# Where the operands of the matmuls lie in SBUF: moving tiles at 416 modulo 1024, weight parts at 0 modulo 1024

## The chip, the core and the metric

The kernel runs on one core of one Trainium2 chip. The metric is the device time of one execution in microseconds. Before the change three runs took 1342.55, 1343.47 and 1345.52 us; the median is 1343.47.

## What is computed

Two layers of a decoder trunk on 256 tokens of width 1024, batch 1, all in float32. Each layer:

```python
h = h + 0.5 * swiglu(rms_norm(h), ffn1)                  # 1024 -> 2 x 2816 -> 1024
u = rms_norm(h)
parts = split(u @ w_in)                                  # q, k, v, gates of four mixers
ys = (gated_deltanet, mlstm, s5_ssm, moba_attention)     # each 256 wide
h = h + sum_b(sigmoid(u @ w_gate[b]) * (ys[b] @ w_branch[b])) @ w_out
h = h + 0.5 * swiglu(rms_norm(h), ffn2)
h = h + (p[i] @ w_ple) * sigmoid(rms_norm(h) @ w_ple_gate)
```

and a final RMSNorm. Most of the arithmetic is in the dense products with w_gu, w_down, w_in, w_gate, w_branch, w_out and w_ple. With 256 tokens each weight is used once per execution, so all weights (some 230 MB) are read from HBM once.

## The kernel before

**Layout.** Activations stand transposed: channels on the 128 partitions, the 256 tokens along the free axis. A dense product takes a 128x128 block of weights as TensorE's stationary operand and a 128x256 block of activations as its moving operand, and writes a 128x256 block of PSUM. For the few products whose result is wanted with tokens on the partitions (`proj_t`: z, av, mv, mo) the roles are swapped: a block of activations is stationary and a block of weights moves.

**Three matmuls for one product.** A float32 number is split in a high part that the fast fp32r format holds exactly and a low part, the rest. A product is then high x high + high x low + low x high, three fp32r matmuls, in `mm3`:

```python
mm(out, w[0], x[0], start=start, stop=False)   # wh stationary, x high moves
mm(out, w[0], x[1], start=False, stop=False)   # wh again, x low moves
mm(out, w[1], x[0], start=False, stop=stop)    # wl stationary, x high moves
```

Every matmul loads its own stationary block (LDWEIGHTS), so there are as many loads as matmuls.

**Weights.** `unit` brings 512 KB of weights with one DMA into a tile `raw` (128 x 1024 float32, 4 buffers); ScalarE casts it into `wh`, VectorE subtracts and writes `wl` (6 buffers each). A block of 128 columns is 512 bytes of a partition's row, so in a unit the eight blocks begin at the tile's start and every 512 bytes after it.

**Moving tiles.** `xa` (two constants, high and low, 8 blocks each) holds the normalised input of a feed-forward network or of the mixers; `A` holds the gated hidden block of a feed-forward network (input of w_down); `B` the merged mixer output (input of w_out), the input of the ple gate and one mixer's result; `Y` and `D` the results of the other mixers, `Y` also the ple embedding. Each 128x256 block is 1024 bytes long, and blocks of a tile follow one another, so all blocks of one tile name begin at the same address modulo 1024.

**The feed-forward loop** (`ffn`): for each of 22 blocks f of the hidden width, 48 matmuls with `xa` moving (gate and up: 2 outputs x 8 blocks x 3), then, two blocks late, 24 matmuls with `A` moving (down: 8 outputs x 3). It runs twice per layer.

**Order.** The kernel records every operation, and a planner (`Plan.order`) puts them in order with a cost per instruction, due times and the number of buffers per tag; `Plan.issue` then emits them all from one line, L427 of the profile. The planner does not know addresses. Its only trace of them is in `cost`, where an fp32r matmul gets 7 ns on top of its columns if the moving tile is `xa`, else 11.

**Addresses.** Tiles are laid out pool by pool in the order in which the pools are opened, in a pool by first use. Before, the order is: 16384 bytes of scratch for DMA descriptors, the constants (`xa` among them), the weights, then all work tiles.

Of the kernel before, what the change touches and what calls it, by code (L numbers as in the profile page):

```python
# [9 lines left out]
F = mybir.dt.float32  # L10
R = mybir.dt.float32r
# [5 lines left out]
T = 256  # L17
D = 1024
KD = D // 128
# [26 lines left out]
def constants():  # L46
# [35 lines left out]
    for name in CONSTS:  # L82
# [3 lines left out]
        parts.append(a)  # L86
    return np.concatenate(parts, axis=1), off


COLS = {"n1": (0, 8), "nm": (8, 8), "n2": (16, 8), "np": (24, 8), "conv": (32, 40), "gb": (72, 1), "alog": (73, 1),  # L90
        "bglu": (74, 2), "d5": (76, 8)}
# [8 lines left out]
BUFS = dict(A=4, B=8, C=8, D=8, T=4, Y=4, M=4, th=4, q=8, sg=2, sq=2, nacc=2, rs=2, tiny=6, rcol=2, s5prm=1, s5s=16,  # L100
            s5pw=1, s5u=2, mv=1, cols=1, gnw=1, mnw=1, sm8=16)


class Store:


    def __init__(self, pool, shape, dt, tag, bufs, bank):
        self.pool, self.shape, self.dt, self.tag, self.bufs, self.bank = pool, shape, dt, tag, bufs, bank
        self.real, self.place, self.end, self.left, self.log = None, None, 0.0, 0, []
# [121 lines left out]
class Plan:  # L231
# [89 lines left out]
    def order(self):  # L321
# [13 lines left out]
        while True:  # L335
            best = None
            for e in names:
                if ready[e]:
                    t = free[e]
                elif later[e]:  # L340
                    t = max(free[e], later[e][0][0])
                else:
                    continue
                if best is None or t < best[0]:
                    best = (t, e)
            if best is None:
                break
            t, e = best
            while t >= tick + TICK:
                warm, count, tick = count >= COLUMNS, 0.0, tick + TICK  # L350
# [54 lines left out]
            for s in v.stores:  # L405
                s.left -= 1
                s.end = max(s.end, v.end + OUT[e])
                if s.left == 0:
                    key = (id(s.pool), s.tag)
                    heapq.heappush(places[key], s.end)  # L410
                    for u in stuck.pop(key, []):
                        u.ready = max(u.ready, t)
                        known(u)
# [60 lines left out]
class Trunk:  # L474
    def __init__(self, ctx, tc, ins, out, off, where):
        self.where = where
        self.tc, self.nc, self.ins, self.out = tc, Plan(tc), ins, out
        E = ctx.enter_context
        self.cp = E(tc.tile_pool(name="const", bufs=1))
        self.wp = E(tc.tile_pool(name="weights", bufs=1))  # L480
        self.tp = E(tc.tile_pool(name="work", bufs=1))
        self.pp = E(tc.tile_pool(name="psum", bufs=1, space=bass.MemoryType.PSUM))
        self.dp = E(tc.tile_pool(name="scratch", bufs=1, space=bass.MemoryType.DRAM))
        nc = self.nc
        self.zr = self.const([128, 128], R, "zr")
        nc.gpsimd.memset(self.zr.bitcast(F), 0.0)
        n = DEPTH * NCOL
        self.xc = self.const([128, n + KD * T], F, "xc")
        self.cols = self.xc[:, 0:n].rearrange("p (l c) -> p l c", l=DEPTH)
        self.h = self.xc[:, n:].rearrange("p (k t) -> p k t", k=KD)  # L490
        self.xa = [self.const([128, KD, T], R, f"xa{j}") for j in range(2)]
        self.start()
        cst = self.const([128, sum(w for _, w in off.values())], F, "cst")
        nc.sync.dma_start(cst[:, 0:128], ins["consts"][:, 0:128])
        self.fcol = self.const([128, KD], F, "fcol")
        with nc.later():
            nc.sync.dma_start(cst[:, 128:], ins["consts"][:, 128:])
            nc.sync.dma_start(self.fcol, ins["final"])
        self.c = {k: cst[:, a:a + w] for k, (a, w) in off.items()}
        self.ident = self.c["ident"]  # L500
        V, P = nc.vector, nc.gpsimd
        self.halfs = self.const([128, 16], F, "halfs")
        P.memset(self.halfs[:, 0:8], -0.5)
        P.memset(self.halfs[:, 8:16], 0.5)
        self.meancol = self.const([128, 1], F, "meancol")
        P.memset(self.meancol, 1.0 / D)
        self.bias = self.const([128, 2], F, "bias")
        P.memset(self.bias[:, 0:1], HALF_PI)
        P.memset(self.bias[:, 1:2], EPS)
        self.pick = self.const([128, 8], R, "pick")  # L510
        with nc.later():
            nc.scalar.copy(self.pick, self.c["pick"])
# [37 lines left out]
        return self.nc.tile(self.pp, shape, F, tag, BANKS[tag], True)  # L550

    def t(self, tag, shape, dt=F):
        return self.nc.tile(self.tp, shape, dt, tag, BUFS[tag])

    def col(self, i, name):
        a, w = COLS[name]
# [1122 lines left out]
```

## Time and profile before

| | |
|---|---|
| median of three runs | 1343.47 us |
| the profiled execution | 1343.09 us |
| its span, first to last instruction | 1341.3 us |
| TensorE busy | 1321.4 us, 99% |
| weight loads busy (beside the matmuls) | 1300.2 us, 97% |
| VectorE, ScalarE, GpSimd busy | 1003.4, 738.7, 39.2 us |
| DMA | 233.67 MB, 174 GB/s in the mean |
| mean granted TensorE clock | 0.994 |

How to read it: the rows further down are of this one execution. PE is TensorE's matmuls, PEld its weight loads, DVE VectorE, ACT ScalarE. A tile pair such as `mm<-A,wh` is the output and its inputs, for a matmul the moving and the stationary tile. Matmuls overlap in the pipeline and their ends are modelled, so the mean length of one is far more than the time from one start to the next; how fast a stream of matmuls runs is seen from a window that holds nothing else, its length divided by the number of matmuls that start in it.

### The profile page before, as it was taken

How to read it: one execution, taken by the hardware profiler on the slowest of the kernel's cores; microseconds unless marked ns; L12 is line 12 of the kernel's file. 1: busy time of each engine (PE TensorE's matmuls, PEld its weight loads, DVE VectorE, ACT ScalarE, POOL GpSimd, SP SyncE). 2: the span in 40 equal slices, each digit the busy share in tenths (PEclk: the TensorE clock that was granted, in tenths of full speed). 3: DMA queues.
4: the chain of work that ended last, by engine and by line, in shares of the span. 5: the costliest groups of instructions: out<-in, count | busy, mean ns of one | idle time of the engine just before them, and what ended most of it. 6: DMA issues, size and time to landing. Idle time of an engine off the chain costs nothing.

```text
span 1341.3 us, 27989 instructions
## 1 busy us (share of the span) xinstructions
PE 1321.4 (99%) x11366; PEld 1300.2 (97%) x11366; DVE 1003.4 (75%) x1893; ACT 738.7 (55%) x1174; POOL 39.2 (3%) x73
## 2 busy tenths in 40 slices
PE   8999999999999999999999999999989999999997
PEld 8999999988999999999999999999989999999997
DVE  7998567987858765556899966778886777555575
ACT  7645457974455544444664454689635455444453
POOL 2000000000010000000020000000000100000000
PEclk9999999998999999999999999999999999999999
DMA  8665555435735655555576645553456356566551
GB/s 296 193 193 163 190 189 173 142 119 115 214 109 178 192 184 189 190 191 200 167 214 190 193 153 189 175 179 103 136 155 205 117 180 194 194 194 192 192 166 60
DMA packets 81761, 233.67 MB, mean 174 GB/s; under 512 B 20832, under 2 KB 24928, under 8 KB 81632
## 3 DMA queue, kind: packets, MB, share of 16 engines
q1 hardware_dynamic: 81632, 231.88, 55.0%
q8 instruction: 89, 1.46, 0.5%
q14 instruction: 40, 0.33, 0.1%
HBM read 229.49 MB, written 2.36 MB: 173 GB/s over the span
## 4 chain that ended last, share of the span: by engine, by line
PE 90%; DMA 3%; issue 2%; ACT 2%; DVE 1%; SPq 0%; POOL 0%; DVEq 0%; POOLq 0%; ACTq 0%
PE mm L427 64%; PE acc L427 19%; PE inv L427 7%; DMA raw<-in_weights 2%; DVE wl L427 1%; ACT wh L427 1%; DMA q<-dx 1%; DMA raw<-dm 0%; SPq L427 0%; DMA xc<-in_x 0%; ACT B L427 0%; ACT C L427 0%; DMA dx<-sg 0%; DVE th L427 0%; DVE D L427 0%
## 5 line engine op out<-in xcount | busy, mean ns | idle before, releaser
L427 PE MATMUL mm<-xa,wh 128*128 128x256 f32 x4288 | 755.4, 279 | 0.4 <-ACT wh L427 0.3
L427 ACT CAST wh<-raw 128x1024 fp32r<-128x1024 f32 (+1 forms) x434 | 437.1, 1038 | 471.4 <-issue 223.0
L427 PEld LDWEIGHTS mm<-xa,wh 128*128 128x128 f32 x4288 | 652.8, 189 | 3.9 <-ACT wh L427 1.0
L427 PE MATMUL mm<-xa,wl 128*128 128x256 f32 x2144 | 597.0, 278 | 0.8 <-DVE wl L427 0.8
L427 DVE TENSOR_TENSOR wl<-raw,wh 128x1024 fp32r<-128x1024 f32 (+1 forms) x434 | 514.2, 1207 | 54.1 <-ACT wh L427 52.9
L427 PEld LDWEIGHTS mm<-xa,wl 128*128 128x128 f32 x2144 | 405.0, 189 | 2.4 <-DVE wl L427 1.4
L427 DVE TENSOR_TENSOR T<-mm,rs 128x512 f32<-128x512 f32 x98 | 67.4, 689 | 168.6 <-PE mm L427 167.1
L427 PE MATMUL acc<-A,wh 128*128 128x256 f32 x1056 | 190.8, 280 | 1.7 <-ACT A L427 1.7
L427 PEld LDWEIGHTS acc<-A,wh 128*128 128x128 f32 x1056 | 161.2, 188 | 2.1 <-ACT A L427 1.9
L427 PE MATMUL acc<-A,wl 128*128 128x256 f32 x528 | 147.2, 280 | 0.0
L427 PE MATMUL mm<-B,wh 128*128 128x256 f32 x576 | 105.1, 283 | 0.0
L427 PEld LDWEIGHTS acc<-A,wl 128*128 128x128 f32 x528 | 99.3, 188 | 0.0
L427 PEld LDWEIGHTS mm<-B,wh 128*128 128x128 f32 x576 | 89.7, 191 | 0.0
L427 PE MATMUL mm<-B,wl 128*128 128x256 f32 x288 | 81.5, 285 | 0.0
L427 PE MATMUL inv<-A,wh 128*128 128x256 f32 x352 | 66.6, 280 | 0.0
L427 PEld LDWEIGHTS mm<-B,wl 128*128 128x128 f32 x288 | 54.9, 191 | 0.0
L427 PEld LDWEIGHTS inv<-A,wh 128*128 128x128 f32 x352 | 54.1, 188 | 0.0
L427 DVE TENSOR_TENSOR th<-mm,rs 128x512 f32<-128x512 f32 (+1 forms) x41 | 27.6, 676 | 31.2 <-PE mm L427 27.6
L427 PE MATMUL mm<-wh,xa 128*128 128x256 f32 (+1 forms) x256 | 49.1, 285 | 0.0
L427 PE MATMUL inv<-A,wl 128*128 128x256 f32 x176 | 49.1, 279 | 0.0
L427 ACT CAST A<-sg 128x256 fp32r<-128x256 f32 x88 | 35.2, 401 | 10.2 <-DVE sg L427 10.2
L427 PEld LDWEIGHTS mm<-wh,xa 128*128 128x128 f32 x256 | 40.1, 188 | 0.7
(263 smaller groups left out, 1351.1 us busy)
## 6 DMA issues: line engine op xcount, KB each, us to landing
raw<-in_weights SPq DMA_DIRECT2D x420, 512.0 KB, 4.3
raw<-in_weights SPq DMA_DIRECT2D x8, 256.0 KB, 5.3
raw<-in_weights SPq DMA_DIRECT2D x4, 408.0 KB, 3.3
dm<-D SPq DMA_DIRECT2D x4, 256.0 KB, 4.5
raw<-dm SPq DMA_DIRECT2D x16, 64.0 KB, 4.4
out_t<-T SPq DMA_DIRECT2D x4, 256.0 KB, 2.5
xc<-in_x SPq DMA_DIRECT2D x3, 256.0 KB, 4.6
raw<-in_weights SPq DMA_DIRECT2D x2, 272.0 KB, 3.0
```

Source lines behind the costliest of these rows:

```text
L427: getattr(getattr(nc, v.engine), v.name)(*map(real, v.args), **{k: real(x) for k, x in v.kw.items()})
```

## The change

Three pools and one size change. No instruction is added or dropped, and on every engine the instructions stand in the same order before and after.

```diff
+OPERANDS = ("A", "B", "Y", "D")
+BASE, WBASE = 288, 768
...
+        self.op = E(tc.tile_pool(name="operands", bufs=1))
+        self.op.tile([128, BASE // 4], F, tag="pad", name="pad")
         self.cp = E(tc.tile_pool(name="const", bufs=1))
         self.wp = E(tc.tile_pool(name="weights", bufs=1))
+        self.wp.tile([128, WBASE // 4], F, tag="pad", name="pad")
...
-        self.xa = [self.const([128, KD, T], R, f"xa{j}") for j in range(2)]
+        self.xa = [nc.tile(self.op, [128, KD, T], R, f"xa{j}") for j in range(2)]
...
     def t(self, tag, shape, dt=F):
-        return self.nc.tile(self.tp, shape, dt, tag, BUFS[tag])
+        return self.nc.tile(self.op if tag in OPERANDS else self.tp, shape, dt, tag, BUFS[tag])
...
-    nc = bacc.Bacc("TRN2", target_bir_lowering=False, num_devices=1)
+    nc = bacc.Bacc("TRN2", target_bir_lowering=False, num_devices=1, dynamic_dma_scratch_size=1024)
```

The pads hold nothing; they only push what follows. The smaller scratch makes room for them. The addresses that come out, in bytes of a partition's row modulo 1024:

| tile | role | before | after |
|---|---|---|---|
| xa | moving; stationary in the row projections (at this and 512 more) | 416 | 416 |
| A | moving | 640 | 416 |
| B | moving | 224 | 416 |
| Y | moving | 416 | 416 |
| D | moving | 576 | 416 |
| wh, wl | stationary, blocks alternate between two addresses | 992, 480 | 0, 512 |
| wh, wl in the row projections | moving, blocks of 256 columns | 992 | 0 |
| raw | read by ScalarE and VectorE, written by DMA | 992 | 0 |
| C | work tile | 640 | 672 |

(In the one row projection that is 272 columns wide the moving blocks begin at 992, 32 and 96 before, and at 0, 64 and 128 after.)

## Rows read from the trace of the kernel before

**Rows 1.** The page, busy time of TensorE and its weight loads.
```profile
PE 1321.4 (99%) x11366; PEld 1300.2 (97%) x11366; DVE 1003.4 (75%) x1893; ACT 738.7 (55%) x1174; POOL 39.2 (3%) x73
```
**Rows 2.** The page, chain that ended last, by engine.
```profile
PE 90%; DMA 3%; issue 2%; ACT 2%; DVE 1%; SPq 0%; POOL 0%; DVEq 0%; POOLq 0%; ACTq 0%
```
**Rows 3.** Windows: mixer outputs to branches, and layer 1's second feed-forward network.
```profile
core 0: us, PE busy (x) PEld busy (x) DVE busy (x) ACT busy (x) POOL busy (x), PEclk, DMA share, GB/s
...
330.00:470.00 140.00, 139.25 (x1260) 137.36 (x1259) 106.83 (x180) 72.04 (x114) 4.88 (x3) 1.00 0.57 174
470.00:640.00 170.00, 170.00 (x1479) 170.00 (x1479) 103.83 (x128) 76.69 (x105) 0.00 (x0) 1.00 0.58 192
```
**Rows 4.** The page, groups: shapes and count, then busy us, mean ns of one.
```profile
L427 PE MATMUL mm<-xa,wh 128*128 128x256 f32 x4288 | 755.4, 279 | 0.4 <-ACT wh L427 0.3
...
L427 PE MATMUL mm<-xa,wl 128*128 128x256 f32 x2144 | 597.0, 278 | 0.8 <-DVE wl L427 0.8
...
L427 PE MATMUL acc<-A,wh 128*128 128x256 f32 x1056 | 190.8, 280 | 1.7 <-ACT A L427 1.7
...
L427 PE MATMUL mm<-B,wh 128*128 128x256 f32 x576 | 105.1, 283 | 0.0
...
L427 PE MATMUL inv<-A,wh 128*128 128x256 f32 x352 | 66.6, 280 | 0.0
```
**Rows 5.** Groups of TensorE by line, the smaller ones.
```profile
L427 PE MATMUL mm<-wh,xa 128*128 128x256 f32 (+1 forms) x256 | 49.1, 285 | 0.0
...
L427 PE MATMUL mm<-wl,xa 128*128 128x256 f32 (+1 forms) x128 | 36.6, 286 | 0.0
L427 PE MATMUL mm<-Y,wh 128*128 128x256 f32 x128 | 23.5, 281 | 0.0
...
L427 PE MATMUL acc<-xa,wh 128*128 128x256 f32 x64 | 12.6, 283 | 0.1
L427 PE MATMUL mm<-D,wh 128*128 128x256 f32 x64 | 12.0, 281 | 0.0
L427 PE MATMUL acc<-Y,wh 128*128 128x256 f32 x64 | 11.6, 279 | 0.0
```
**Rows 6.** Windows, matmuls on xa, three blocks of 48, each behind a block of A.
```profile
core 0: us, PE busy (x), PEclk, DMA share, GB/s
39.15:44.62 5.47, 5.47 (x48) 1.00 0.76 268
...
128.28:133.93 5.65, 5.65 (x48) 1.00 0.76 245
136.75:142.19 5.44, 5.44 (x48) 1.00 0.84 282
```
**Rows 7.** Windows, matmuls on A, two blocks of the first feed-forward network.
```profile
36.34:39.15 2.81, 2.81 (x24) 1.00 0.18 31
44.62:47.44 2.82, 2.82 (x24) 1.00 0.60 203
```
**Rows 8.** Windows, matmuls on Y, one block of a branch.
```profile
334.19:336.91 2.72, 2.72 (x24) 1.00 0.51 173
```
**Rows 9.** Windows, matmuls on D, one block of a branch.
```profile
406.88:409.75 2.87, 2.87 (x24) 1.00 0.81 216
```
**Rows 10.** Windows, matmuls on B, the last branch's end and the output product.
```profile
432.37:458.27 25.90, 25.90 (x216) 1.00 0.61 186
```
**Rows 11.** Windows, the same 48-matmul row projection in both layers (two earlier matmuls counted).
```profile
244.70:250.15 5.45, 5.45 (x50) 1.00 0.54 181
905.63:911.28 5.65, 5.65 (x50) 1.00 0.57 204
```
**Rows 12.** Timeline: start us, us, what; twelve fp32 matmuls of 64 columns.
```profile
224.39 1.45 PE L427 MATMUL acc<-C,B 128*128 128x64 f32 x12
225.65 0.48 PE L427 MATMUL mm<-xa,wh 128*128 128x256 f32 x2
```
**Rows 13.** The page, the data queue: packets, MB, share of 16 engines.
```profile
q1 hardware_dynamic: 81632, 231.88, 55.0%
```

## The prediction

> **What bounds the kernel now.** I read the page's busy line first, then the chain, then the stages. TensorE is busy for 1321.4 of 1341.3 us [rows 1] and 90% of the chain that ended last is TensorE's own work [rows 2]. In the second feed-forward network of a layer it never rests: 170.00 us busy out of 170.00, at a granted clock of 1.00 (the 2.4 GHz level), while VectorE has 103.83, ScalarE 76.69 and the DMA engines a share of 0.58 [rows 3]. So here the time is a count of matmuls times the step from one matmul's start to the next, which I call the pitch. No row prints it. A matmul shows about 280 ns because matmuls overlap, so the pitch has to be a window's length divided by the matmuls that begin in it.
>
> The reader should see in [rows 6 to 10] that the same instruction (128x128 stationary, 256 moving columns) has several pitches, by the tile that moves. xa: 5.44 us for 48, 113.3 ns, at best [rows 6]. Y: 2.72 for 24, 113.3 [rows 8]. A: 2.81 and 2.82 for 24, 117.3 [rows 7]. D: 2.87 for 24, 119.6 [rows 9]. B: 25.90 for 216, 119.9 [rows 10]. The granted clock is 1.00 in all of them, and the DMA share does not order them (Y 0.51, B 0.61, slow A 0.18). What orders them is the address: xa and Y are the two tiles that begin at 416 modulo 1024, and they are the two fast ones.
>
> **The change part by part.** It adds and drops no instruction and moves none; every engine has the same list in the same order. Two things change: where A, B and D lie (from 640, 224 and 576 to 416), and where every stationary tile lies (from 992 and 480 to 0 and 512).
>
> *Moving tiles.* I price them first as if the moving address alone decided, so that each goes to 113.3 ns. Counts: two thirds of a group use wh, one third wl, as in 4288 and 2144 for xa [rows 4]. A has 1056 + 352 with wh, so 2112 in all: 2112 x (117.3 - 113.3) = 8.4 us. B has 576, so 864: 864 x (119.9 - 113.3) = 5.7 us. D has 64, so 96 [rows 5]: 96 x (119.6 - 113.3) = 0.6 us. There is a fourth term: each xa block of these networks follows a block of A, and takes 5.47 us where the best takes 5.44 [rows 6]; I read the difference as the time in which the stream finds its short step again after A's. Behind a block of equal pitch that goes (the Y blocks come straight after xa blocks and have 113.3 throughout, [rows 8]): 88 blocks (22 per network, 2 networks, 2 layers) x 0.03 = 2.6 us. Sum 17.3 us, all of it on TensorE and on the path, since TensorE is full where A and B are used. TensorE would then want its inputs 1.3% sooner; the shares of the others in [rows 3] leave room for that, so nothing is late next.
>
> *Stationary tiles.* 9888 matmuls have wh or wl as stationary operand (xa 6528 with the 96 of the s5 projection, A 2112, B 864, Y 288, D 96), and no row of before has them at 0 and 512. One ns is worth 9.9 us here, so this is the term that decides. Bounds: the longest pitch of this form is B's 119.9, the shortest step with a full weight load that I find is 1.26 us for 12 fp32 matmuls of 64 columns, 105 ns [rows 12]. All at 119.9 would cost xa 6528 x 5.9 = 38.5 and A 5.5 us; all at 105 would give back some 80. Between ends this far apart I take the nearest row. Measured as moving start minus stationary start modulo 512, before has xa and Y at 448, A at 160, B at 256, D at 96; after has 416 for all of them. That is 32 bytes from the 113.3 of xa and Y and 160 or more from the others. So I take 113.3, and no gain beyond it.
>
> *The row projections.* There wh and wl move and xa is stationary: 992 against 416 and 928 before, 0 against the same after; 288 matmuls of 256 columns and 96 of 272 ([rows 5]: 256 + 128). The same 48-matmul projection has 5.45 us in the first layer and 5.65 in the second [rows 11], so it sits at either pitch, 113.5 or 117.7. Bounds: all at 119.6, +1.2 us; all at 113.5, -0.6. I take 0.
>
> *The rest.* The smaller scratch is the one for descriptors of the other kind of DMA; all data goes through the hardware queue [rows 13], so this costs nothing. Vector, scalar and DMA operands land on other addresses too; whatever that does is covered in the feed-forward stages by the idle third of VectorE and half of ScalarE [rows 3].
>
> So the forecast is 1343.1 (the profiled execution, span 1341.3) - 17.3 = 1325.8; the median of the runs is 0.4 above that execution, so 1326.2.
>
> **Rivals.** *First, and serious: the distance decides, with a period of 128 bytes, and the new distance is a bad one (slower).* For it: an address alone does not fix the pitch. xa at 416 has blocks of 5.44 us and blocks of 5.65 us [rows 6], with the same instructions and addresses, so two streams must be falling in and out of step. And the row projections, moving at 992, show the same two values [rows 11]. What they share with xa is the distance modulo 128: 448 and 64 are both 64. A is at 32, D at 96, B at 0. After the change everything is at 416 = 32 modulo 128, where A is now: 117.3. Price: xa 6528 x (117.3 - 114.0) = 21.5, Y 288 x 4.0 = 1.2, B 864 x -2.6 = -2.2, D -0.2, row projections (96 modulo 128, as D is) +1.2: +21.5 us, 1365. It decides from the point where xa's pitch passes 116.6, since 2.6 ns on 6528 eats the 17 us. If the class were B's, 1343.5 + 38.5 + 5.5 + 1.9 + 1.2 = 1390. Against it: the period is read from two classes only, and modulo 256 or 512 the new distance is another class or none seen.
>
> *Second: addresses do nothing, the pitch comes from something else in each stage.* Then 1343.5. Against it: Y and B stand in the same stage, with 113.3 and 119.9 [rows 8, 10].
> The Trainium skill speaks for this rival and so against the change: its page "SBUF — State Buffer", section "Who interferes with whom", gives TensorE two independent read ports, one for the moving operand and one for weight loads, and says that it never waits on anyone. By that rule an operand's address could not matter and the sum would be 0; the two pitches of [rows 8, 10] disagree with it.
>
> *Third: the weights at 0 and 512 no longer lie across a 1024-byte line, and the pitch falls below 113.3 for all.* The step of 105 ns in [rows 12] shows that a load does not need 113. One to two ns on 9888 are 10 to 20 us more: about 1310.
> The Trainium skill, "TensorE: Matmul & The Clock Gate", section "Back-to-back issue gap", gives N/2.4 + 2.5 ns for a warm matmul, an estimate of 109.2 ns for 256 columns; by it another 4 ns, 40 us, would be to be had; no row of this form comes under 113.
>
> **How the numbers follow.** Forecast (everything near 113.3; its own range 1317 to 1331, from the first three terms or less up to a few slow xa blocks gained as well) 43%; a mixture of the two pitches, 1331 to 1341, 6%; third rival 7%; second 7%; first rival at A's pitch or less, 1346 to 1368, 24%; worse than that 13%. A measurement of this kernel tells no change to about 0.2%, 2.7 us. So faster 43 + 6 + 7 = 56%, same 7%, slower 37%. The range leaves out some 6% below 1317 and 13% above 1368.
>
> **What would show it.** In the profile after: 24 matmuls on A in 2.72 us and 216 on B in 24.5 us for the moving tiles; 48 on xa in 5.44 us right after an A block for the weights and the fourth term. Blocks of 5.63 us on xa with 2.81 on A would be the first rival; 2.81 on A and 25.9 on B, the second; xa under 5.4, the third. The forecast is wrong if xa's pitch moves by more than a nanosecond, whatever A and B do.

## The result and the profile after

The changed kernel takes 1356.36 us (median of four runs, 1355.88 to 1356.86) against 1344.28 us before (four runs, 1342.55 to 1345.52): a ratio of 1.0094, 95% interval 1.0079 to 1.0109. It is 12.1 us slower; 17.3 us faster had been forecast. The profiled execution took 1356.01 us with a span of 1354.2, 12.9 us more than the one before, and it is this one that the rows show.

First the page of the changed kernel: busy time, the chain, and the groups of matmuls (shapes and count, then busy us and mean ns of one). The planner's line is L430 now.

```profile
PE 1340.4 (99%) x11366; PEld 1319.6 (97%) x11366; DVE 1004.7 (74%) x1893; ACT 738.4 (55%) x1174; POOL 39.1 (3%) x73
...
PE 93%; issue 2%; DMA 2%; ACT 1%; DVE 1%; SPq 1%; POOL 0%; DVEq 0%; POOLq 0%; ACTq 0%
...
L430 PE MATMUL mm<-xa,wh 128*128 128x256 f32 x4288 | 774.8, 282 | 0.4 <-ACT wh L430 0.3
...
L430 PE MATMUL mm<-xa,wl 128*128 128x256 f32 x2144 | 603.1, 281 | 0.5 <-DVE wl L430 0.5
...
L430 PE MATMUL mm<-B,wh 128*128 128x256 f32 x576 | 103.3, 280 | 0.0
```

Against [rows 1, 2, 4]: the same instructions, TensorE busy 19.0 us longer, VectorE and ScalarE as before to 1.3 us. Both groups on xa grew (755.4 to 774.8 and 597.0 to 603.1), B's fell by 1.8. The two windows of [rows 3], with the same columns:

```profile
330.00:470.00 140.00, 140.00 (x1249) 138.19 (x1248) 105.83 (x178) 70.64 (x112) 4.88 (x3) 1.00 0.56 174
470.00:640.00 170.00, 170.00 (x1451) 170.00 (x1450) 101.40 (x125) 76.10 (x105) 0.00 (x0) 1.00 0.58 186
```

In the same 170 us of a feed-forward network TensorE now starts 1451 matmuls where it started 1479, with no rest and at the same clock of 1.00. So the step from one matmul to the next became longer here, and no wait was added. Whose step, the windows by moving tile show (us, busy and count, clock, DMA share, GB/s): two blocks of 48 on xa, the row projection in both layers; two blocks of A; then Y, D and B.

```profile
38.48:44.12 5.64, 5.64 (x48) 1.00 0.79 261
129.31:135.00 5.69, 5.69 (x48) 1.00 0.75 245
248.54:254.30 5.76, 5.76 (x50) 1.00 0.61 204
913.76:919.52 5.76, 5.76 (x50) 1.00 0.59 194
...
35.67:38.48 2.81, 2.81 (x24) 1.00 0.16 25
135.00:137.85 2.85, 2.85 (x24) 1.00 0.12 47
...
333.42:336.24 2.82, 2.82 (x24) 1.00 0.39 150
...
406.91:409.73 2.82, 2.82 (x24) 1.00 0.81 227
...
432.96:458.30 25.34, 25.34 (x216) 1.00 0.60 189
```

Divided by their matmuls (0.01 us of a window is 0.2 to 0.4 ns): xa 117.5 ns where it had 114.0 behind a block of A [rows 6], Y 117.5 (113.3, [rows 8]), D 117.5 (119.6, [rows 9]), B 117.3 (119.9, [rows 10]), and A 117.1 as ever [rows 7]. All five tiles have one pitch, the one that A alone had: it is longer for xa and Y and shorter for B and D. In part of the feed-forward blocks (129 us and on) both tiles run at 118.5 to 118.8. The row projections, whose distance is now 96 modulo 128, went to 5.76 us (50 matmuls counted, two of them earlier ones), 120.0 ns for 48, from 5.45 and 5.65 [rows 11].

On xa 3.3 to 3.5 ns on 6528 matmuls is 22 us, and the span grew by 12.9. Part of it is given back in the mixers, where TensorE waits for VectorE's D. TensorE's waits of the whole span (for what, us in total, times, longest), the kernel before and the changed one:

```profile
PE acc L427 <- DVE D L427: 6.6, 2, 3.4
```
```profile
PE acc L430 <- DVE D L430: 2.5, 2, 1.8
```

TensorE around this wait in the first layer, from the same matmul on Y to the same block of Y, before and after (us, busy and count, clock, DMA share, GB/s):

```profile
313.48:318.94 5.46, 2.33 (x20) 1.00 1.05 206
318.94:334.19 15.25, 15.25 (x104) 0.78 0.35 108
```
```profile
317.85:320.95 3.10, 2.38 (x20) 1.00 0.82 303
320.95:333.42 12.47, 12.47 (x104) 1.00 0.48 137
```

The changed kernel reaches this place 4.4 us late (317.85 against 313.48) and leaves it 0.8 us early (333.42 against 334.19). It waits 0.72 us in place of 3.13, and the 104 instructions behind the wait take 12.47 us at a clock of 1.00 where they took 15.25 at 0.78. (Between the two levels of 1.00 and 0.50, 2.4 and 1.2 GHz, a mean of 0.78 is an estimate of 6.7 us at the lower one.) An estimate of the whole from these rows: 22 us for xa, 1.2 for Y and 1.3 for the row projections, less 2.4 for B and D, less 2.8 for the clock behind this wait, less 6.5 for all of TensorE's waits (13.3 us before, 6.8 after, by the same view; those for D are 4.1 of it), which comes to 12.8.

Two things could shorten the wait: a TensorE that comes later, or a D that is ready sooner. The chain of waits (start us, us, what) has one piece ahead of D that changed its length, a 64 KB transfer of rows into a `raw` tile; before, then after:

```profile
311.15 5.62 DMA raw<-dm
```
```profile
315.29 3.50 DMA raw<-dm
```

The median time to landing of all 16 such transfers is 4.4 us before and 3.5 after, by the page's list of DMA issues (KB each, us to landing):

```profile
raw<-dm SPq DMA_DIRECT2D x16, 64.0 KB, 4.4
```
```profile
raw<-dm SPq DMA_DIRECT2D x16, 64.0 KB, 3.5
```

### The profile page after: what moved, and what is told of

It is laid out like the page before. It is cut to its first block, busy times and chain, and to the rows that moved or that the text cites. A ratio compares the mean times of both kernels' runs of the same rounds, so it can differ in the third digit from the quotient of the medians.

```text
span 1354.2 us, 27989 instructions
## 1 busy us (share of the span) xinstructions
PE 1340.4 (99%) x11366; PEld 1319.6 (97%) x11366; DVE 1004.7 (74%) x1893; ACT 738.4 (55%) x1174; POOL 39.1 (3%) x73
## 4 chain that ended last, share of the span: by engine, by line
PE 93%; issue 2%; DMA 2%; ACT 1%; DVE 1%; SPq 1%; POOL 0%; DVEq 0%; POOLq 0%; ACTq 0%
PE mm L430 66%; PE acc L430 19%; PE inv L430 7%; DMA raw<-in_weights 1%; DVE wl L430 1%; SPq L430 1%; ACT wh L430 1%; DMA raw<-dm 1%; DMA q<-dx 0%; ACT B L430 0%; POOL rcol L430 0%; ACT sq L430 0%; DVEq L1681 0%; ACT L430 0%; DVE th L430 0%
## 5 line engine op out<-in xcount | busy, mean ns | idle before, releaser
L430 PE MATMUL mm<-xa,wh 128*128 128x256 f32 x4288 | 774.8, 282 | 0.4 <-ACT wh L430 0.3
L430 ACT CAST wh<-raw 128x1024 fp32r<-128x1024 f32 (+1 forms) x434 | 436.7, 1037 | 485.2 <-issue 235.2
L430 PEld LDWEIGHTS mm<-xa,wh 128*128 128x128 f32 x4288 | 659.0, 189 | 3.7 <-ACT wh L430 0.8
L430 PE MATMUL mm<-xa,wl 128*128 128x256 f32 x2144 | 603.1, 281 | 0.5 <-DVE wl L430 0.5
L430 DVE TENSOR_TENSOR wl<-raw,wh 128x1024 fp32r<-128x1024 f32 (+1 forms) x434 | 514.3, 1208 | 52.1 <-ACT wh L430 51.0
L430 PEld LDWEIGHTS mm<-xa,wl 128*128 128x128 f32 x2144 | 404.2, 189 | 2.3 <-DVE wl L430 1.1
L430 DVE TENSOR_TENSOR T<-mm,rs 128x512 f32<-128x512 f32 x98 | 67.5, 690 | 182.5 <-PE mm L430 180.6
L430 PE MATMUL acc<-A,wh 128*128 128x256 f32 x1056 | 191.2, 280 | 0.9 <-ACT A L430 0.9
L430 PEld LDWEIGHTS acc<-A,wh 128*128 128x128 f32 x1056 | 161.7, 188 | 1.3 <-ACT A L430 1.1
L430 PE MATMUL acc<-A,wl 128*128 128x256 f32 x528 | 147.4, 280 | 0.0
L430 PE MATMUL mm<-B,wh 128*128 128x256 f32 x576 | 103.3, 280 | 0.0
L430 PEld LDWEIGHTS acc<-A,wl 128*128 128x128 f32 x528 | 99.4, 188 | 0.0
L430 PEld LDWEIGHTS mm<-B,wh 128*128 128x128 f32 x576 | 88.2, 188 | 0.0
L430 PE MATMUL mm<-B,wl 128*128 128x256 f32 x288 | 80.7, 282 | 0.0
L430 PE MATMUL inv<-A,wh 128*128 128x256 f32 x352 | 66.7, 280 | 0.0
L430 PEld LDWEIGHTS inv<-A,wh 128*128 128x128 f32 x352 | 54.2, 188 | 0.0
L430 PEld LDWEIGHTS mm<-B,wl 128*128 128x128 f32 x288 | 54.1, 188 | 0.0
L430 DVE TENSOR_TENSOR th<-mm,rs 128x512 f32<-128x512 f32 (+1 forms) x41 | 27.6, 676 | 34.1 <-PE mm L430 30.2
L430 PE MATMUL mm<-wh,xa 128*128 128x256 f32 (+1 forms) x256 | 49.9, 287 | 0.0
L430 PE MATMUL inv<-A,wl 128*128 128x256 f32 x176 | 49.3, 280 | 0.0
L430 PEld LDWEIGHTS mm<-wh,xa 128*128 128x128 f32 x256 | 40.4, 188 | 0.7
```

The lines of the kernel that those rows point to most:

```text
L430: getattr(getattr(nc, v.engine), v.name)(*map(real, v.args), **{k: real(x) for k, x in v.kw.items()})
```

## Experiments

Two theories stood after the result. *Distance:* the pitch is set by moving start minus stationary start, with a period of 128 bytes. *Address:* the new places of the weights (or of the tiles) are bad by themselves. Each edit is shown against the changed kernel, if nothing else is said; WBASE and BASE are the pads ahead of the weights and of the moving tiles. "Freed" below is a block of xa near 113.5 ns behind a block of another pitch. A measured time is the median of four runs, with the lowest and the highest, if no other number of runs is given; the ratio is to the kernel before, run beside it.

### The weights back at 992, all moving tiles at 416 (distance 448)

```diff
-BASE, WBASE = 288, 768
+BASE, WBASE = 288, 736
```


> The changed kernel with the weights' parts back at 992 and 480 modulo 1024; xa, A, B, Y and D stay at 416. Distance theory (the pitch is set by moving start minus stationary start modulo 128: 64 gives 113.3 ns, 32 gives 117.3, 0 and 96 some 119.9): every moving tile is at 64, so A 24 in 2.72 us, B 216 in 24.5 us, xa 48 in 5.44 us; about 1327 us by the matmuls' sum, up to 1332 if the mixers' serial parts give back some of it. Rival, the weights' place does not matter and the five tiles themselves are slow where they now lie: as the changed kernel, 1356.

Measured: 1337.45 us (1333.66 to 1350.24, ten runs), ratio 0.9969 (0.9941 to 0.9997). Three windows of xa in the slowest of these runs, which is the profiled one:

```profile
38.46:43.90 5.44, 5.44 (x48) 1.00 0.78 240
128.11:133.76 5.65, 5.65 (x48) 1.00 0.72 243
136.59:142.24 5.65, 5.65 (x48) 1.00 0.85 266
```

113.3 ns at first, and from about 125 us on 117.7, for xa and A alike and through the rest of this feed-forward network (in this run 60 of the 80 blocks of exactly 48 matmuls on xa are slow, 20 fast). At this distance there are two pitches, and a stream stays for long in the one that it is in. The runs are spread over 17 us. That the two pitches are the reason is not shown, since only the slowest run was traced, but they are large enough: 60 blocks of xa and 59 of the 80 of A at 4.4 ns more per matmul are an estimate of 19 us. The median lies 5 to 10 us above the 1327 to 1332 expected. So moving the weights is what costs in the change; whether by their distance or by their place, the next runs tell. With A at xa's distance, nothing in the loop brings the stream back.

### The moving tiles at 576, the weights at 0 (distance 64 modulo 512)

```diff
-BASE, WBASE = 288, 768
+BASE, WBASE = 448, 608
```


> The changed kernel with the five moving tiles at 576 modulo 1024, the weights still at 0 and 512. 576 is where D was slowest before (119.6 ns). Distance theory with period 128: 576 is 64 modulo 128, so all at 113.3 ns and the row projections (0 against 576: 64) at 113.5 to 117.7; 1327 to 1332 us. Rival, weights at 0 and 512 are slow for any moving tile: 117 ns or more, 1356 or slower. Rival, the moving address decides by itself: 119.6 ns for all, about 1376. Rival, the distance counts but with period 512 (576 is 64 there, never seen with these roles): open.

Measured: 1353.11 us (1348.13 to 1354.51), 1.0069 (1.0046 to 1.0093). A window of xa:

```profile
38.45:44.10 5.65, 5.65 (x48) 1.00 0.79 262
```

117.7 ns, the slow pitch of distance 448, in 79 of the 80 blocks of 48 on xa. The 1327 to 1332 us expected of the period of 128 did not come: 64 and 448 share their pitches, but not how often the fast one is held.

### The kernel before with only the weights moved

```diff
         self.wp = E(tc.tile_pool(name="weights", bufs=1))
+        self.wp.tile([128, 8], F, tag="pad", name="pad")
```

This edit is against the kernel before. All work tiles move by 32 bytes with the weights, so that of the moving tiles only xa's distance changes, from 448 to 416 (the row projections, where xa is stationary, change with it, and `raw` comes to 0).

> The kernel before with a pad of 32 bytes ahead of the weights alone: weights at 0 and 512, and all work tiles 32 further as well, so that only xa's distance changes (64 to 32 modulo 128) while A, B, Y, D keep theirs. Distance theory: xa 117.3 ns (48 in 5.63 us), A 117.3, B 119.9, D 119.6, Y still 113.3 (24 in 2.72 us); 1344 + 6528 x 3.3 ns = 1366 less what shorter waits take back (the changed kernel's sum was 21.5 and its time rose by 12): 1357 to 1366. Rival, weights at 0 and 512 are slow for any moving tile: Y at 117 or more as well.

Measured: 1356.34 us (1355.33 to 1359.32), 1.0104 (1.0086 to 1.0122), the time of the whole change. Windows of xa, of Y (distance still 448) and of B (still 256):

```profile
38.83:44.46 5.63, 5.63 (x48) 1.00 0.77 266
...
348.12:350.85 2.73, 2.73 (x24) 1.00 0.41 156
...
434.13:460.04 25.91, 25.91 (x216) 1.00 0.61 190
```

xa is at 117.3, Y, with its weights at 0 and 512 too, keeps 113.8, B keeps 119.9. An address that is bad by itself falls: the same weight places give three pitches by the distance.

### Distances 0, 48 and 80

```diff
-BASE, WBASE = 288, 768
+BASE, WBASE = 384, 672
```


> The changed kernel with the five moving tiles at 512 modulo 1024, weights at 0 and 512: distance 0. Distance theory: B's pitch of before for all, 119.9 ns, xa 48 in 5.76 us; 9888 x 2.6 ns = 25 us over the changed kernel, 1375 to 1382 us. Rival, a start on a 512-byte line is the best place for a stream: 113 or less, under 1332 us.

For distances that are no multiple of 32 the moving operand is a slice 16 bytes into a longer tile (for 48 with pads of 256 and 768, for 80 of 288 and 736):

```diff
+OFF = 16 // 4
...
+        x = self.nc.tile(self.op, [128, n + 32], dt, tag, bufs)[:, OFF:OFF + n]
```


> All five moving tiles start 48 bytes (modulo 128) after the stationary start, a distance between 32 (117.3 ns, one state) and 64 (113.3 and 117.8, two states that last until something disturbs the stream). If the period is 128 with steps of 32 bytes, it behaves as one of its two neighbours: 117.3 everywhere (1356 us) or both states (1333 to 1350). If the pitch follows the distance finely, it may have a single state between 113.3 and 117.3 and then a steady time between 1328 and 1350.

> The same at 80 bytes, between 64 (two states) and 96 (119.6 to 119.9, one state). Steps of 32 bytes: two states (1333 to 1350 us) or 119.7 everywhere (about 1376). A fine dependence: a single state in between.

Measured: distance 0: 1376.82 us (1374.48 to 1378.26), 1.0248 (1.0228 to 1.0268). Distance 48: 1364.63 us (1362.43 to 1366.4), 1.0158 (1.0137 to 1.018). Distance 80: 1378.2 us (1377.74 to 1378.55), 1.026 (1.0241 to 1.0279). One window of xa each:

```profile
38.58:44.34 5.76, 5.76 (x48) 1.00 0.82 262
```
```profile
38.34:43.99 5.65, 5.65 (x48) 1.00 0.79 270
```
```profile
38.62:44.38 5.76, 5.76 (x48) 1.00 0.79 265
```

120.0, 117.7 and 120.0 ns. At distance 0 all tiles have B's old pitch. Of the distances modulo 128 that were tried only 64 has blocks near 113.3 ns, and 16 bytes to either side they are gone.

At 48 and 80 the other tiles do not all have xa's pitch. The longer tiles start at several places modulo 512 and keep their distance modulo 128 alone, and A's blocks have two pitches in either run, by their windows 118.3 and 119.6 ns at 48, 118.3 and 119.2 at 80 (two blocks of each run):

```profile
35.50:38.34 2.84, 2.84 (x24) 1.00 0.05 7
43.99:46.86 2.87, 2.87 (x24) 1.00 0.54 196
```
```profile
35.78:38.62 2.84, 2.84 (x24) 1.00 0.01 3
44.38:47.24 2.86, 2.86 (x24) 1.00 0.62 199
```

So the distance modulo 128 alone does not fix the pitch here either; that the second pitch belongs to buffers 128 bytes apart modulo 256 would fit, but is not shown.

### A apart, at a distance of its own

First with the weights at 992 and A at 640, so that xa (448) and A (32 modulo 128) stand as before and only B, Y and D are moved:

```diff
-OPERANDS = ("A", "B", "Y", "D")
-BASE, WBASE = 288, 768
+OPERANDS = ("B", "Y", "D")
+BASE, WBASE = 288, 512
...
+        self.hp = E(tc.tile_pool(name="hidden", bufs=1))
+        self.hp.tile([128, 224 // 4], F, tag="pad", name="pad")
```


> The kernel with weights at 992 and xa, B, Y, D at 416 (distance 64), but A back at 640 (distance 32). Memory theory (at distance 64 a stream stays at 113.3 or 117.8, whichever it fell into, until a wait or a block at another distance; a block of A at distance 32 brings the next xa block to 113.3 within some five matmuls): xa 48 in 5.47 us behind every A block, A 24 in 2.82, as before the change, B and D at 113.3 or 117.8: 6 us at most for these, so 1337 to 1341 us with a small spread, against 1333 to 1350 with A at 416 too. Rival, the two values of that run have another cause (the pool's place, the run): xa in both values here as well, with the same wide spread.

Measured: 1339.66 us (1337.25 to 1341.66, ten runs), 0.9973 (0.996 to 0.9985). Three windows of xa, then one of D:

```profile
38.73:44.21 5.48, 5.48 (x48) 1.00 0.67 189
129.13:134.78 5.65, 5.64 (x48) 1.00 0.77 246
137.60:143.05 5.45, 5.45 (x48) 1.00 0.82 276
...
405.50:408.22 2.72, 2.72 (x24) 1.00 0.83 235
```

The block at 129 us has fallen to 117.7 ns; behind the next block of A, xa is back at 113.5. With all tiles at one distance the slow stretch went on from there. A's place at another distance is what kept the kernel before near 113.5. D at 448 has 113.3. The gain is in the spread: the highest of ten runs is 8.6 us lower than with A at 416, while the median, 1339.66 against 1337.45, is no better, since A's own matmuls stay at the longer step.

The same with xa, B, Y and D at 576, weights at 0 and A at 672 (pads 448, 512 and 96):

> The kernel with weights at 0 and xa, B, Y, D at 576 (distance 64 modulo 128, 64 modulo 512), where all blocks ran at 117.8 ns, but A at 672 (distance 32). Memory theory with period 128: the A blocks now free the xa blocks, 48 in 5.47 us, A 24 in 2.82; 1337 to 1341 us. Rival, at this place (weights on a 512-byte line) distance 64 has only the slow pitch: xa stays at 5.65, 1350 us or more.

Measured: 1353.18 us (1351.79 to 1355.77), 1.0076 (1.0054 to 1.0097).

```profile
38.47:44.12 5.65, 5.65 (x48) 1.00 0.86 263
137.94:143.59 5.65, 5.65 (x48) 1.00 0.79 278
```

Here A frees nothing: xa stays at 117.7 ns behind A. My theory, which knew only the period of 128, failed; two ways out were left: the weights' place (32 off a multiple of 64, as 992 is), or a longer period for which of the two pitches is entered.

### Distance 448 at other places

Weights at 32, xa at 480, A at 576; then weights at 64, xa at 512, A at 608 (pads 352 and 384, with 640 and 96):

> Weights at 32 and 544 modulo 1024, xa, B, Y, D at 480 (distance 64 modulo 128), A at 576 (distance 32). The distances are those of the next kernel; what differs is that the weights begin 32 bytes off a 64-byte line and not on one. Alignment theory (with the weights 32 off a 64-byte line, as at 992 and 480, a block of A frees xa to 113.3; on a line, as at 0 and 512, xa stays at 117.8): xa 48 in 5.47 us, 1338 to 1341 us. Rival, the place 992 itself or some longer period matters: xa at 117.8, 1353 us.

> The same with everything 32 further: weights at 64 and 576, on a 64-byte line, xa, B, Y, D at 512 and A at 608. Alignment theory: as with weights at 0 and xa at 576, xa 48 in 5.65 us, 1350 to 1356 us. Rival (the distance alone counts): as the kernel with weights at 32.

Measured: 1337.23 us (1335.04 to 1340.78, seven runs), 0.9961 (0.9945 to 0.9976), and 1336.13 us (1334.28 to 1337.84), 0.9946 (0.9927 to 0.9965). A window of xa of each:

```profile
38.26:43.72 5.46, 5.46 (x48) 1.00 0.65 206
```
```profile
38.57:44.02 5.45, 5.45 (x48) 1.00 0.76 266
```

Freed at both places, 113.5 to 113.8 ns. The weights' place falls once more; the distance stays.

The changed kernel with everything moved by 32 bytes (pads 320 and 768: moving tiles at 448, weights at 32 and 544) is the counterpart:

> The changed kernel with all moving tiles and the weights 32 bytes further (448; 32 and 544): the same distances in other places. If the distance alone counts for the pitch at 32: 117.3 ns, 1356 us. If the alignment of the weights to 64 bytes counts here as well: another pitch than the changed kernel's, with the weights off the line as A had before the change, 117.3 in one state; so 1354 to 1357 either way unless distance 32 has a further state.

Measured: 1361.47 us (1360.54 to 1362.65), 1.0135 (1.0117 to 1.0154).

```profile
38.17:43.80 5.63, 5.63 (x48) 1.00 0.78 263
128.94:134.63 5.69, 5.69 (x48) 1.00 0.77 258
```

The same two steps as in the changed kernel, 117.3 and 118.5 ns, at other addresses. It is nonetheless 5 us slower than the changed kernel, and slower than expected. Its transfers `raw<-dm` take 4.6 us in the median, and TensorE waits for D nearly as long as before, 5.7 us for 6.6:

```profile
PE acc L430 <- DVE D L430: 5.7, 2, 3.2
```

TensorE comes to this wait late here too, by 4.0 us in the first layer, so that is not what shortens it; `raw` at 32 in place of 0 is what is left. Over the traces it is a clean divide: where `raw` begins at 0 modulo 512, the transfers land in 3.4 to 3.8 us and the waits for D are 2.4 to 3.7 us; where it begins at 32, 64, 224 or 992, 4.2 to 4.8 us and 5.6 to 6.6 us, at every pitch.

### Distance 192: a period of 256 or of 512

Weights at 0, xa, B, Y and D at 192, A at 288 (pads 64, 896 and 96). 192 and 448 are the same modulo 256, 64 is not.

> Weights at 0 and 512, xa, B, Y and D at 192 (distance 192 modulo 512, which is 64 modulo 128 and 448 modulo 256), A at 288 (32 modulo 256). Theory of a period of 256: behaves as the runs with distance 448: about 75 of xa's 48-column-block runs at 113.3 to 114.0 ns, A near 116.8, time 1334 to 1340 us. Rival, period 512 (only 448 is freed): xa stays at 117.7 to 117.8 as at 576, time 1350 to 1355 us. Rival, the place itself (192 is another place of the partition): anything outside both.

Measured: 1332.52 us (1331.63 to 1333.89), 0.9919 (0.9896 to 0.9941). A window of xa and one of Y:

```profile
38.54:43.99 5.45, 5.45 (x48) 1.00 0.84 249
...
329.20:332.02 2.82, 2.82 (x24) 1.00 0.30 112
```

Freed: 113.5 ns behind A's blocks, with weights at the very places of the change. So 192 and 448, one class modulo 256, behave alike, and a period of 512 falls; 320, the fellow of 64, was not tried. Against the run with xa at 576, xa moved from 64 to 192 modulo 256 and A from 160 to 32. A at 160 does free xa at 192 (the first run of this kind, weights at 992); xa at 64 with A at 32 was not run. In the mixers of this run, where no A comes by, Y and xa run at 117.5 ns: the slow pitch exists here as well. The run is 3.6 us under the one at 448 with weights at 64, and under the 1334 to 1340 expected; this goes with `raw`: 3.6 us per transfer and 3.4 us of waits for D, against 4.2 and 5.7.

### `raw` alone at 0

The kernel before, with `raw` in a pool of its own ahead of the constants; every other tile keeps its place modulo 1024 (the pads add up to 1024):

```diff
+        self.rp = E(tc.tile_pool(name="raws", bufs=1))
+        self.rp.tile([128, 896 // 4], F, tag="pad", name="pad")
...
-        return (nc.tile(self.wp, [128, 1024], F, "raw", RAW_BUFS),
+        return (nc.tile(self.rp, [128, 1024], F, "raw", RAW_BUFS),
```


> The kernel before with raw alone moved, from 992 to 0 modulo 1024; every other tile keeps its place modulo 1024, so every distance between moving and stationary operands stays. Theory of the target: the small transfers raw<-dm land in 3.4 to 3.8 us (4.4 before), TensorE's waits for VectorE's D fall from 6.6 to 3 to 4.5 us, and the time falls by 2 to 6 us, 1338 to 1342, at xa's 114.0 ns. Rival, TensorE waits less only because its longer pitch makes it come late: transfers and waits as before, 1342 to 1345 us. Second rival, it is wh and wl (or another tile) whose place matters to the transfer's neighbours: also 1342 to 1345, and then the runs with wh and wl at 0 keep an unexplained gain.

Measured: 1335.44 us (1333.52 to 1337.89, six runs), 0.9951 (0.9932 to 0.9969): 6.6 us (4.2 to 9.1) faster by the place of one tile that no matmul reads. The same piece of the chain, then TensorE's waits for D:

```profile
310.32 3.44 DMA raw<-dm
```
```profile
PE acc L427 <- DVE D L427: 3.5, 2, 2.5
```

3.44 us for 5.62, and 3.5 us of waits for 6.6; A and xa keep their pitches (117.3 and 114.0 ns). The work behind the first of these waits gains as well: the wait is 0.95 us for 3.13, and the same 104 instructions take 12.12 us at a clock of 1.00 for 15.25 at 0.78:

```profile
315.93:328.05 12.12, 12.12 (x104) 1.00 0.50 145
```

Waits and clock together are 6.2 us, about the whole gain. It is the gain that the changed kernel has in the mixers, and both rivals fall.

### Every fourth block of A apart

If one block of A frees the stream, not all of them have to pay for it: one in four goes to a buffer A2 at distance 32, the rest stay at xa's distance. First with weights at 992 (A2 at 640), then with weights at 64 (A2 at 608), at last with weights and `raw` at 0 and distance 192 (A2 at 288):

```diff
-            act2 = self.t("A", [128, 2, T], R)
+            act2 = self.t("A2" if f % 4 == 3 else "A", [128, 2, T], R)
```


> Weights at 992, xa, B, Y, D at 416 and of the hidden blocks A three in four at 416 too, every fourth at 640 (distance 32) in a tile of its own. Memory theory: one block at distance 32 in four rounds is enough to bring the stream back to 113.3 after a wait, and the other 66 of 88 A blocks gain 24 x 4.0 ns and the next xa block its 0.03 us: 6.3 + 2.0 us less than with all A at 640, 1331 to 1334 us with a small spread. Rival, a single block does not free the stream often enough: spread as with all at 416, 1333 to 1350.

> The places of the run with weights at 64 (distance 448), but only every fourth hidden block A stands at 608 (distance 32), the others at 512 (distance 448). Theory of two pitches with memory: xa and A at 113.3 most of the time, the block apart alone at 116.8; if each block apart brings the stream back, the time is that of the run with all of A apart less 18 of 24 blocks of A x (116.8 - 113.3) ns per matmul, at most 5 to 8 us less: 1329 to 1336 us. Rival, memory lasts shorter than four blocks: as the mixed run at 416 and 640, 14 or more of xa's blocks at 117.8, time 1336 to 1340 us.

> Weights and raw at 0, xa, B, Y, D and three of four hidden blocks A at 192, every fourth block at 288. Theory: distance 192 is freed by one block in four as 448 was, and raw at 0 gives the shorter transfers: the time of the run with all of A at 288 (1332.5) less up to 5 us, 1327 to 1333. Rival: at 192 the stream falls into 117.7 ns more often when three of four blocks stand at the same distance, which eats the saving: 1332 to 1337.

Measured: 1337.2 us (1332.2 to 1340.47, nine runs), 0.9951 (0.9933 to 0.9968); 1332.05 us (1330.01 to 1335.72), 0.9919 (0.9895 to 0.9943); 1329.45 us (1326.53 to 1330.97, six runs), 0.99 (0.9883 to 0.9917). In the first of the three, xa ahead of a block of A2 and behind it:

```profile
144.57:150.22 5.65, 5.65 (x48) 1.00 0.81 262
...
169.69:175.13 5.44, 5.44 (x48) 1.00 0.86 278
```

117.7 ns until the block of A2 (at 158.70 us), 113.3 ns behind it: 24 matmuls freed the stream for the rest of this network. The first run still missed the 1331 to 1334 us and the small spread expected of it: in its trace 13 of the 80 blocks on xa are slow, in the other two 11 and 10, against 3 or 4 in the traces with all of A apart at distances 448 and 192. So part of what A gains is paid by xa. Each of the three has a median 2.5 to 4.1 us under its fellow with all of A apart; the intervals of each pair overlap, so that this gain is likely and not shown for any one pair. The last has the lowest median of this study, 13.4 us under the kernel before (11.1 to 15.7); it joins the three things that the runs point to, distance 192, a block apart, and `raw` at 0.

## Why the prediction was wrong

**The step that failed** is the term of the stationary tiles. The prediction measured distances modulo 512, found 416 nearest to the 448 of xa and Y, and took 113.3 ns by "the nearest row". The runs showed 117.3 to 118.6 ns there, some 22 us on xa's 6528 matmuls where the sum had none. Nearness means little here: 416 is 32 modulo 128, and the runs give, by the distance modulo 128, 0 → 120.0 ns, 32 → 116.8 to 118.6, 48 → 117.7 to 119.6, 64 → 113.3 or 117.7, 80 → 118.3 to 120.0, 96 → 119.6 to 120.0 (D before, the row projections after). 16 bytes off the best distance cost 4 to 7 ns. The prediction had this period in hand, as its first rival, and set it behind because it had been read from too few classes.

**The moving tiles.** "As if the moving address alone decided" fell with it. A's 8.4 us did not come (117 ns before and after), and the fourth term turned round: xa's blocks are not freed of A's step, all of them have it. The reading under that term was thin as well: the block of 5.44 us in [rows 6] stands behind a block of A like the one of 5.47. Of B's 5.7 us 2.2 came (25.34 for 25.90 us on 216 matmuls, a quarter of the 864), of D's 0.6 some 0.2. The pitch that these terms hoped for is there at distance 448: D's 24 matmuls took 2.72 us with the weights at 992.

**The row projections**, taken as 0, went to 120.0 ns in the windows shown, as the first rival said: on 288 matmuls against the mean of the two windows before (115.6) 1.3 us.

**"The rest", costed at nothing**, was a gain of 6.6 us (4.2 to 9.1). The prediction covered the new addresses of DMA operands by idle time in the feed-forward stages; but the transfers into `raw` that matter are those of the mixers, where TensorE waits behind them, and in the sum by queue [rows 13] they are lost among the 232 MB of the weights.

**The first rival** was the case that came: 5.63 us on xa with 2.81 on A was its mark, 5.64 and 2.81 were seen. Its price of 21.5 us is a little too high for what it speaks of: with `raw` not at 0 the same distances cost 18.1 us (1.0135 on 1342.4; 15.7 to 20.7), for it counted matmuls alone, and all of TensorE's waits are 3.1 us shorter in that trace (10.2 for 13.3). The change as it stands costs 12.1, since it moves `raw` to 0 as well: 18.1 - 6.6 = 11.5.

**The other rivals.** That addresses do nothing fell with every run. The Trainium skill's page "SBUF — State Buffer", section "Who interferes with whom", calls TensorE's two read ports independent, one for the moving operand and one for weight loads; 113.3 to 120.0 ns by the distance of just these two operands, at one clock, disagree. A pitch below 113.3 for weights at multiples of 512 did not come: no block of 24 or more matmuls in any trace is under it.

**Open.** What in the chip makes the distance count, how a stream falls into the slow one of two pitches, and why 64 modulo 256 keeps it where 192 is freed, is described here and not explained. 64 modulo 256 is not always slow: the first layer's row projection before stood at it, with the roles swapped, and had 113.5 [rows 11]. Nor is it shown why the place of `raw` makes a transfer of 64 KB up to 2 us longer. It writes 512 pieces of 128 bytes, which lie across a multiple of 128 at 32, 64, 224 and 992 and not at 0; whether that is the reason, and whether other multiples of 128 would do, was not tried.

## What to carry to other kernels

Where TensorE is full and each matmul loads its own weights (seen here for fp32r, 128x128 stationary and 256 moving columns), work out moving start minus stationary start modulo 128 and 256 for every pair of tiles, and measure the pitch of each class from windows before any tile is moved; one address for all is no aim in itself. Give the tile with the most matmuls the class with the short step (192 modulo 256 here), and keep a block of another class in its stream: with 192 modulo 256 it brought the short step back after a disturbance, with 64 it did not. When tiles are moved, every reader and writer moves with them: look also at the transfers into them that stand in a chain of waits.

## What was not expected of the hardware

- The same matmul takes 113.3 to 120.0 ns by the distance of its two operands within a partition's row, at a clock of 1.00.
- At distance 64 modulo 128 two pitches keep themselves up: in one run 48 matmuls on xa took 5.44 us in one stretch and 5.65 in another. 24 matmuls at another distance end the slow one at 192 modulo 256 (5.65 us ahead, 5.44 behind), not at 64 (5.65 us behind as well). At 32 there are two as well (5.63 and 5.69 us).
- 64 KB in 512 pieces of 128 bytes landed in 3.4 to 3.8 us (median of 16) with the target at 0 modulo 512, in 4.2 to 4.8 at 32, 64, 224 and 992.
- After a wait of 3.13 us the granted clock was 0.78 in the mean of the next 15 us; after one of 0.72 us, at the same place of the program, 1.00.
